# Projection A of a hybrid decoder layer as seven products of half blocks, with double-width evictions and a merge by halves of the tokens

## The chip, the cores and the metric

The kernel runs on one core of a Trainium2 chip. A core has a matrix engine (TensorE, PE in the profile; its weight loads are listed apart as PEld), a vector engine (VectorE, DVE), an activation engine (ScalarE, ACT), GpSimd (POOL) and a queue engine (SyncE, SP) that here only issues DMAs. Each engine works through its own list of instructions in order and waits on semaphores for the others. The metric is the device time of one execution in microseconds. Three runs of the kernel before took 1434.97, 1435.62 and 1437.99 us; the median is 1435.62 us.

## The reference, cut to what matters

One layer of a decoder trunk is computed for a prompt of 1024 tokens and for eight samples of one token, together 1032 columns. All data is float32.

```
h = rmsnorm(x, norm_pre) * (1 + scale) + shift
hA, cA, bA, zA, qkv, zB, beta_raw, alpha_raw, gA, gB = split(h @ w_in)
yA = ((bA * conv3(cA * hA)) * silu(zA)) @ w_out_a      # branch A, "projection A"
o  = gated_delta_rule(conv4(qkv), ...)                 # branch B, eight heads
yB = (rmsnorm(o) * silu(zB)) @ w_out_b                 # "projection B"
merged = sigmoid(gA) * yA + sigmoid(gB) * yB
y = x + gate * rmsnorm(merged @ w_o, norm_post)        # gate: from c @ ada_w, the "row gate"
```

The states of both convolutions and of the delta rule are outputs too.

## The kernel before, in words

Activations lie transposed: 128 channels on the partitions, 1032 tokens along the row (NT). A matrix of 1024 channels is eight such tiles. To keep float32 accuracy, each operand is split into a high part (a cast to float32r, on ACT) and a low part (the difference, on DVE), and each product of two tiles is three matmuls: high by high, high by low, low by high.

The stages, in order of time: a start with the norms; `run(jobs, 1, isp)`, the eight heads with the gates gA and gB, and the first three channel tiles of branch A; `products()`, the input tiles 3 to 7 of branch A; `products_b()`, projection B; `run(jobs, ioa, len(jobs))`, projection A; and the loop over nine row tiles with w_o, the last norm and the outputs. Results that a later stage needs (yA and yB before their projections, both gates) lie in DRAM: `yAsc`, `yBsc`, `gAsc`, `gBsc`.

`products()` and `products_b()` use the scheme of Strassen and Winograd on 2 x 2 blocks: a pair of output tiles by two halves of the tokens (HT = 516 columns) is made of seven products P1, P2, P6, P7, P4, P5, P3 (in that order), each of half as many input tiles. A product is taken in two pieces of PW = 258 columns, 12 matmuls each, and each piece is evicted from its PSUM bank by `evacuate`: ACT copies P1 to two quarters, DVE adds the others (two additions for P5, one for the rest). The weights of the products, some of them sums of blocks, are prepared by `weight_load` and `weight_gen`, one unit ahead; the operands of projection B by `yblock_gen`, at most three products ahead, from raw rows (P1, P2, P3) or from sums that `park_gen` has written to the DRAM tile `txs` (P6, P7, P4, P5), which come back through POOL's queue. In projection B a unit is a product with one of two weight groups; each unit serves two pairs of tiles.

Projection A before is plain: eight jobs, one for each output tile, of three groups of 344 columns and eight input tiles, three matmuls each. `load_rows` loads and splits the eight rows of yA, `oa_evac` multiplies each group by the sigmoid of gA and adds it to `mrg`, which holds the gated yB. While it runs, `side_gen` writes the convolution state of branch A and computes the row gate (32 matmuls of 512 columns, `rowgate_gen`), and `wo_gen` loads and splits w_o, tile by tile. The w_o loop starts with the sample tile (8 rows, `order = [8] + ...`), then the eight prompt tiles; `prep(j)` loads x and splits the columns of `mrg` for tile j, one tile ahead.

The order of instructions on each engine is written by a small planner while the program is built. Background work is a list of generators (strands). Between matmuls `slot()` advances every strand whose due time, worked out from costs written in the code, lies 450 ns behind the planner's clock of PE; `force(cond)` advances strands, and the clock with them, until a condition holds. A strand yields after each step, so that the next engine's step is written later. Nothing is reordered on the chip: an engine that comes to an instruction waits there. Buffers of a row's size come from a list (`T4`, 6 at first, 22 more for the products, 7 more from projection B on); `take` forces one free, `ready(n)` lets a strand wait for n. PSUM is eight banks in two pools of four.

Of the kernel before, what the change touches and what calls it, by code (L numbers as in the profile page):

```python
# [153 lines left out]
def hybrid_step(  # L154
# [22 lines left out]

    def tt(out, a, b, op):
        V.tensor_tensor(out=out, in0=a, in1=b, op=op)
# [94 lines left out]
    txs = dram.tile([2, 2, 4, P, NT], F32R, name="txs")  # L274
# [1013 lines left out]
    def conv_state_gen(branch):  # L1288
# [6 lines left out]
        for src, n, nt, o_p, o_s, row in (which,):  # L1295
            for t0 in range(0, nt, 4):
                pt = ps_aux()
# [13 lines left out]
    def rowgate_gen():  # L1311
        pt = [ps_aux(), ps_aux()]
# [34 lines left out]
    def side_gen():  # L1347
        yield from conv_state_gen("a")
        yield from rowgate_gen()

# [33 lines left out]
    UNITS = [(t, p, 0) for t in range(SG, NK) for p in PROD] + [("B", p, g) for p in PROD for g in range(2)]  # L1384

    def weight_load(raw):
        for key in list(range(SG, NK)) + ["B"]:
            w, n = (w_out_b, 2) if key == "B" else (w_in, 1)
            for odd, half in ((0, 0), (0, 1), (1, 0), (1, 1)):
                for g in range(n):  # L1390
                    yield from when(lambda: len(raw) < 4 * n, lambda: T4.ready())
# [38 lines left out]
    def park_gen():  # L1430

        for k in range(4):
            yield from when(lambda: T4.ready(2))
            a, b = T4.get("pa_", NT), T4.get("pb_", NT)
            SY.dma_start(out=a, in_=yBsc[k])
            SY.dma_start(out=b, in_=yBsc[4 + k])
            yield
            a1, a2, b1, b2 = a[:, 0:HT], a[:, HT:NT], b[:, 0:HT], b[:, HT:NT]
            tt(a1, a2, a1, ALU.subtract)
            tt(a2, b2, a2, ALU.subtract)  # L1440
            yield
            tt(b2, b2, a1, ALU.subtract)
            tt(b1, b1, b2, ALU.subtract)
            yield
            for r, v in enumerate((a, b)):
                yield from when(lambda: T4.ready(2))
                hi, lo = T4.get("phi", NT), T4.get("plo", NT)
                A.copy(out=hi.bitcast(F32R), in_=v)
                yield
                tt(lo.bitcast(F32R), v, hi, ALU.subtract)  # L1450
                T4.give(v)
                store(txs[r, 0, k].bitcast(F32), hi)
                store(txs[r, 1, k].bitcast(F32), lo)
                T4.give(hi)
                T4.give(lo)
                yield
        parked.append(True)

    parked = []
    yblk = {}  # L1460

    def yblock_gen():
# [109 lines left out]
    def products():  # L1572
# [3 lines left out]
        for t in range(SG, NK):  # L1576
            tiles = [T4.take("acc", NT) for _ in range(4)]
            for p in PROD:
# [6 lines left out]
                for q in range(2):  # L1585
                    ta, tb = tiles[2 * q:2 * q + 2]
                    for half in range(2):
                        ps = banks[4 * (n % 2) + 2 * q + half]
                        for k in range(4):
# [4 lines left out]
                            if k < 3:  # L1594
                                slot()
# [298 lines left out]
```

## Time and profile before

| | |
|---|---|
| median of three runs | 1435.62 us |
| the profiled execution's own time | 1434.01 us |
| its span, first to last instruction | 1432.3 us |
| mean granted clock of TensorE | 0.998 |
| PE, PEld busy | 98%, 94% of the span |
| DVE, ACT, POOL busy | 69%, 46%, 2% |
| DMA | 111 GB/s on average |
| products, from about 927 to 1147 us with the start of projection B's loads | PE full, DVE 82% up to 1128 us |
| projection B, 1147 to 1228 us | DVE 59.69 us busy |
| projection A, 1227.5 to 1326.7 us | DVE 59.45 us busy |
| w_o, from 1326.7 us | 93.2 us of matmuls without a pause, then 7.7 us to the end |

Times are microseconds unless marked ns, counted from the start of the span. A row of a group gives line, engine, operation, output and input tiles, shapes and count, then the busy time, the mean duration in ns and the idle time before the group with what ended it. All instructions carry the line of the planner's wrapper, L121, so groups are told apart by their tiles. `pm_t` and `pa_t` are the two PSUM pools. Matmuls overlap in the array: the time that one costs is the distance between two starts, not its duration. A few matmul records are missing from the trace.

### The profile page before, as it was taken

The numbers are of one execution on the slowest core, as the hardware profiler recorded it, in microseconds if no ns is written. First come the engines' busy times: TensorE is split into PE (matmuls) and PEld (weight loads), VectorE is DVE, ScalarE is ACT, GpSimd is POOL, SyncE is SP. The second block draws the span as 40 slices with busy tenths as digits, with TensorE's granted clock in tenths as the row PEclk, the third lists the DMA queues.
The fourth block names the chain that finished last, engine by engine and source line by source line (L and its number), as shares of the span: only waits on it lengthen the run. The fifth ranks groups of instructions, "written<-read, shape, count | busy, mean of one in ns | idle before, by whom it ended". The sixth has DMA issues, their size and how long they took to land.

```text
span 1432.3 us, 25802 instructions
## 1 busy us (share of the span) xinstructions
PE 1401.0 (98%) x10130; PEld 1340.5 (94%) x10130; DVE 984.4 (69%) x2436; ACT 656.4 (46%) x1521; POOL 35.6 (2%) x59
## 2 busy tenths in 40 slices
PE   6999999899999999999999999999999999999997
PEld 4899999899999999999999999999999999999786
DVE  6754867759569585496864924988877867854553
ACT  6766453855528554466383332253323344532211
POOL 0000000100001000000000000000000110000000
PEclk9999999999999999999999999999999999999999
DMA  9523143132422324224132221344711885743221
GB/s 320 144 48 102 54 127 81 54 80 78 119 60 69 94 62 117 50 66 121 54 97 68 79 68 32 118 170 164 243 53 42 236 265 172 244 150 91 92 87 59
DMA packets 181922, 158.59 MB, mean 111 GB/s; under 512 B 25351, under 2 KB 157856, under 8 KB 181794
## 3 DMA queue, kind: packets, MB, share of 16 engines
q1 hardware_dynamic: 177248, 148.43, 35.2%
q0 software_dynamic: 4352, 8.46, 2.0%
q8 instruction: 79, 1.29, 0.4%
q14 instruction: 41, 0.34, 0.1%
q10 hardware_dynamic: 202, 0.08, 0.0%
HBM read 120.25 MB, written 36.91 MB: 110 GB/s over the span
## 4 chain that ended last, share of the span: by engine, by line
PE 84%; DVE 8%; DMA 5%; ACT 1%; issue 1%; SPq 1%; DVEq 0%; ACTq 0%
PE pm_t L121 63%; PE pa_t L121 19%; PE pb L121 2%; DVE acc L121 2%; DVE wlo L121 1%; DMA xs<-in_x_prompt_dram 1%; SPq L121 1%; DMA yraw<-yAsc 1%; DVE Tt L121 1%; DVE kq L121 1%; DMA wor<-in_w_o_dram 1%; DVE Ttmp L121 1%; DVE wr L121 0%; DMA yraw<-yBsc 0%; DMA pa__11678<-yBsc 0%
## 5 line engine op out<-in xcount | busy, mean ns | idle before, releaser
L121 PE MATMUL pm_t<-xh,whi 128*128 128x344 f32 (+1 forms) x1576 | 517.9, 329 | 2.2 <-ACT gate L121 2.2
L121 PE MATMUL pm_t<-xh,wlo 128*128 128x344 f32 (+1 forms) x1576 | 500.4, 318 | 0.0
L121 PE MATMUL pm_t<-xl,whi 128*128 128x344 f32 (+1 forms) x1576 | 500.1, 317 | 0.0
L121 PEld LDWEIGHTS pm_t<-xh,whi 128*128 128x128 f32 x1576 | 297.4, 189 | 4.7 <-ACT gate L121 2.5
L121 PEld LDWEIGHTS pm_t<-xl,whi 128*128 128x128 f32 x1576 | 297.3, 189 | 0.2
L121 PEld LDWEIGHTS pm_t<-xh,wlo 128*128 128x128 f32 x1576 | 296.9, 188 | 0.4
L121 DVE TENSOR_TENSOR wlo<-wraw,whi 128x512 fp32r<-128x512 f32 x136 | 91.8, 684 | 65.2 <-ACT whi L121 63.1
L121 ACT CAST whi<-wraw 128x512 fp32r<-128x512 f32 x136 | 82.7, 623 | 85.6 <-PE pm_t L121 83.6
L121 DVE TENSOR_TENSOR Ttmp<-Tt 32x30 f32<-32x30 f32 (+14 forms) x240 | 76.1, 317 | 14.7 <-DMA Tt<-sA 10.3
L121 DVE TENSOR_TENSOR Tt<-Tt,Ttmp 32x30 f32<-32x30 f32 (+14 forms) x240 | 76.2, 317 | 4.4
L121 ACT CAST whi<-wr 128x1024 fp32r<-128x1024 f32 x42 | 44.0, 1047 | 73.5 <-PE pa_t L121 34.9
L121 DVE SCALAR_TENSOR_TENSOR kq<-raw,vecs,kq 128x528 f32<-128x528 f32 x96 | 69.9, 758 | 1.5 <-ACT kq L121 1.3
L121 PE MATMUL pm_t<-thi,wlo 128*128 128x258 f32 x240 | 67.6, 283 | 1.6 <-DVE wlo L121 1.6
L121 PE MATMUL pm_t<-tlo,whi 128*128 128x258 f32 x240 | 67.6, 282 | 0.0
L121 PE MATMUL pm_t<-thi,whi 128*128 128x258 f32 x240 | 67.6, 282 | 0.0
L121 PE MATMUL pa_t<-thi,whi 128*128 128x258 f32 x224 | 63.3, 282 | 1.1 <-ACT whi L121 1.1
L121 PE MATMUL pa_t<-thi,wlo 128*128 128x258 f32 x224 | 63.4, 283 | 0.8 <-DVE wlo L121 0.8
L121 PE MATMUL pa_t<-tlo,whi 128*128 128x258 f32 x224 | 63.2, 282 | 0.0
L121 PE MATMUL pm_t<-yhi,whi 128*128 128x344 f32 x192 | 61.5, 321 | 0.0
L121 PE MATMUL pm_t<-ylo,whi 128*128 128x344 f32 x192 | 61.4, 321 | 0.0
L121 PE MATMUL pm_t<-yhi,wlo 128*128 128x344 f32 x192 | 61.4, 320 | 0.0
L121 DVE TENSOR_TENSOR wlo<-wr,whi 128x1024 fp32r<-128x1024 f32 x42 | 51.3, 1221 | 8.9 <-ACT whi L121 8.7
(406 smaller groups left out, 2834.0 us busy)
## 6 DMA issues: line engine op xcount, KB each, us to landing
wraw<-in_w_in_dram SPq DMA_DIRECT2D x60, 512.0 KB
wr<-in_w_in_dram SPq DMA_DIRECT2D x40, 256.0 KB
aw<-in_ada_w_dram SPq DMA_DIRECT2D x16, 512.0 KB
gBsc<-gate SPq DMA_DIRECT2D x8, 516.0 KB
gAsc<-gate SPq DMA_DIRECT2D x8, 516.0 KB
txs<-phi SPq DMA_DIRECT2D x8, 516.0 KB
txs<-plo SPq DMA_DIRECT2D x8, 516.0 KB
tlo<-txs POOLq DMA_DIRECT2D x8, 516.0 KB, 7.3
```

What stands on the lines that cost most here:

```text
L121: r = f(*args, **kw)
```

## The change

Projection A gets the scheme of projection B: `products_b` becomes `products_y(y)` and runs for "B" and then for "A"; weights, parked sums and operand blocks are made for both, with a DRAM tile `txs` for each. The products of A are accumulated in eight row buffers.

PSUM is divided anew from `products()` on: three tiles of two banks each for the products, and two single banks for the row gate and the state of branch A. Both pieces of a product lie in the two banks of one tile and are evicted by one instruction of 2 x 258 columns (`product`).

The gate of A works by halves of the tokens (`merge_gen`): sigmoid of half a row, product with half an accumulator, addition to `mrg`. The first halves start after P4, the second after P5 and P3.

The row gate moves from projection A into `products()`, behind the parking of B and ahead of the parking of A; the state of branch A moves to P4 of projection A, as does the start of `wo_gen`, which also waits until the last operand block is out. The w_o loop takes the prompt tiles first and the sample tile last; the first four prompt tiles ask only for merged first halves, and leave slots for background work.

```diff
-    def side_gen():
-        yield from conv_state_gen("a")
-        yield from rowgate_gen()
+    def side_gen():
+        for k in range(4):
+            yield from park_gen("B", k)
+        yield from rowgate_gen()
+        for k in range(4):
+            yield from when(lambda: ("yA", 4 + k) in flags)
+            yield from park_gen("A", k)
...
     def products():
-        start(park_gen())
-        banks = [ps_main() for _ in range(4)] + [ps_aux() for _ in range(4)]
+        psum["pm"].release()
+        psum["pa"].release()
+        psum["pp"] = tc.alloc_tile_pool(name="pp", bufs=3, space=PSUM)
+        psum["pr"] = tc.alloc_tile_pool(name="pr", bufs=2, space=PSUM)
+        start(side_gen())
...
+    def product(p, whi, wlo, k0, operands, ta, tb):
+        ps = psum["pp"].tile([P, 2, 512], F32, tag="pp", name="pp")
+        for half in range(2):
+            out = ps[:, half, 0:PW]
+            for k in range(4):
+                xh_, xl_ = operands[4 * half + k]
+                PE.matmul(out, lhsT=whi[:, k0 + k, :], rhs=xh_, start=k == 0, stop=False)
+                PE.matmul(out, lhsT=whi[:, k0 + k, :], rhs=xl_, start=False, stop=False)
+                PE.matmul(out, lhsT=wlo[:, k0 + k, :], rhs=xh_, start=False, stop=k == 3)
+                if k < 3:
+                    slot()
+            if half == 0:
+                slot()
+        v = ps[:, :, 0:PW]
+        C11, C12, C21, C22 = (t_[:, o:o + HT].rearrange("p (h n) -> p h n", h=2) for t_ in (ta, tb) for o in (0, HT))
         if p == "P1":
             A.copy(out=C11, in_=v)
             A.copy(out=C12, in_=v)
         for out, in_ in {"P1": (), "P2": ((C11, C11),), "P6": ((C12, C12),), "P7": ((C22, C12),),
                          "P4": ((C21, C22),), "P5": ((C22, C22), (C12, C12)), "P3": ((C12, C12),)}[p]:
             tt(out, v, in_, ALU.add)
...
+    def merge_gen(t, half):
+        yield from when(lambda: T4.ready())
+        s_ = T4.get("sg", NT)
+        hs = slice(half * HT, half * HT + HT)
+        sg, acc_ = s_[:, 0:HT], T["acc", t][:, hs]
+        SY.dma_start(out=sg, in_=gAsc[t, :, hs])
+        yield
+        act(sg, sg, AF.Sigmoid)
+        yield
+        tt(acc_, acc_, sg, ALU.mult)
+        T4.give(s_)
+        yield from when(lambda: ("gate", t) in flags, lambda: half == 0 or ("merged", t, 0) in flags)
+        tt(T["mrg"][:, t, hs], T["mrg"][:, t, hs], acc_, ALU.add)
+        flags["merged", t, half] = True
+        if half:
+            T4.give(T["acc", t])
+
+    def products_y(y):
         for p in PROD:
             for g in range(2):
...
+                if y == "A" and p == "P4" and g:
+                    start(conv_state_gen("a"))
+                    start(wo_gen())
...
+                    product(p, whi, wlo, 4 * q, xs_, ta, tb)
+                    if y == "B" and p in ("P5", "P3"):
+                        t = 2 * i + (p == "P5")
+                        start(gate_gen(t))
+                    elif y == "A" and p in ("P4", "P5", "P3"):
+                        for t, half in {"P4": ((2 * i, 0), (2 * i + 1, 0)), "P5": ((2 * i + 1, 1),),
+                                        "P3": ((2 * i, 1),)}[p]:
+                            start(merge_gen(t, half))
...
     def wo_gen():
         for t in range(NK):
-            yield from when(lambda: T4.ready(3 if flags.get("rg") else 6))
+            yield from when(lambda: T4.ready(3), lambda: flags.get("yblocks"))
...
-    products_b()
-    run(jobs, ioa, len(jobs))
+    products_y("B")
+    products_y("A")
     force(lambda: flags.get("rg") and all(("wo", t) in T for t in range(NK)))
...
-    order = [8] + list(range(8))
+    order = list(range(8)) + [8]
...
     def prep(j):
         i = order[j]
         n = P if i < 8 else NB
-        xr = S_.get("xr", D)
+        force(lambda: all(("merged", t, int(i > 3)) in flags for t in range(NK)))
+        xr = S_.take("xr", D)
...
+                if j < 4:
+                    slot()
```

More of the change, by code (lines that the diff above doesn't have):

```diff
@@ L1585, in products @@
                 for q in range(2):
[L1586 to L1589, printed above, removed]
[L1590 to L1598 removed]
+                    xs_ = [operand(p, k, half) for half in range(2) for k in range(4)]
+                    product(p, whi, wlo, 4 * q, xs_, *tiles[2 * q:2 * q + 2])
                 if t == NK - 1 and p in ("P6", "P7", "P4"):
```

234 lines of the change are left out of this document (85 added, 149 removed).

## The prediction

> **What bounds the kernel now.** I read the first page for the shares, then a table of stretches for the end of the kernel, then the matmuls, the vector engine and the waits inside these stretches.
>
> ```profile
> span 1432.3 us, 25802 instructions
> PE 1401.0 (98%) x10130; PEld 1340.5 (94%) x10130; DVE 984.4 (69%) x2436; ACT 656.4 (46%) x1521; POOL 35.6 (2%) x59
> 927.00:1128.00 201.00, 199.68 (x1638) 199.15 (x1637) 164.49 (x255) 73.81 (x105) 0.83 (x1) 1.00 0.44 140
> 1147.00:1228.00 81.00, 78.68 (x651) 77.95 (x650) 59.69 (x96) 39.19 (x53) 4.90 (x7) 1.00 0.68 220
> 1227.50:1326.70 99.20, 99.20 (x617) 95.71 (x616) 59.45 (x87) 34.91 (x43) 0.00 (x0) 1.00 0.50 156
> 1326.70:1331.40 4.70, 3.83 (x18) 1.68 (x16) 4.42 (x6) 2.27 (x4) 0.00 (x0) 1.00 0.66 232
> 1331.40:1424.60 93.20, 93.18 (x400) 73.88 (x400) 43.73 (x131) 17.65 (x41) 0.00 (x0) 1.00 0.20 68
> ```
>
> The columns of the stretches: length, then PE, PEld, DVE, ACT and POOL busy, granted clock, DMA share, GB/s. They are the products of branch A's input tiles 3 to 7, projection B, projection A, the seam, and w_o. PE never rests for more than a moment, so time is won only by fewer or shorter matmuls, and lost wherever PE begins to wait. DVE is the second engine: 82% (164.49 of 201) in the products, 74% in projection B, 60% in projection A, 47% in w_o. That last row is what I watch, since the change moves vector work between these stages.
>
> **The matmuls of projection A.** Busy times overlap, so the pace is read from start to start.
>
> ```profile
> 1249.16 0.63 PE L121 MATMUL pa_t<-rg_h,cP 128*64 128x512 f32 x2
> 1249.62 0.63 PE L121 MATMUL pa_t<-rg_l,cP 128*64 128x512 f32 x2
> 1250.09 0.32 PE L121 MATMUL pm_t<-yhi,whi 128*128 128x344 f32 x1
> ...
> 1255.93 0.32 PE L121 MATMUL pm_t<-ylo,whi 128*128 128x344 f32 x1
> 1198.64 5.75 PE pa_t L121 x48
> 1204.39 5.82 PE pm_t L121 x48
> ```
>
> From 1250.09 to 1255.93 are 38 matmuls of 344 columns, 37 steps: 5.84/37 = 157.8 ns. In projection B (the chain's last two rows) 48 matmuls of 258 columns take 1204.39-1198.64 = 5.75 us: 119.8 ns. Removed: 8 tiles x 3 groups x 8 x 3 = 576 x 157.8 ns = 90.9 us. Added: 4 pairs x 7 products x 2 halves x 4 x 3 = 672 x 119.8 ns = 80.5 us. **Saved: 10.4 us.** The columns fall to 7/8 (672 x 258 of 576 x 344), which would be 79.5 us; the shorter matmul costs a little more a column, 0.464 ns against 0.459. The row gate's 32 matmuls (0.93 us for four, 7.4 us) go from this stage into the products: nothing won, nothing lost on PE. The same holds for the transposes of the conv state.
>
> **What DVE has to do at the end of projection A.** The merging of the two branches, which stood spread over the 99 us of projection A, may begin only with product P4, and the splits of w_o only behind P4's first half as well. From there to the first complete w_o tile DVE's price decides. Three rows of projection B give its pace back to back, two more the single durations.
>
> ```profile
> 1207.07 1.42 DVE L121 TENSOR_TENSOR mrg<-pm_t,mrg 128x258 f32<-128x258 f32 x4
> 1208.41 1.22 DVE L121 TENSOR_TENSOR mrg<-mrg,sg 128x1032 f32<-128x1032 f32 x1
> 1209.55 1.46 DVE L121 TENSOR_TENSOR mrg<-pm_t,mrg 128x258 f32<-128x258 f32 x4
> L121 DVE TENSOR_TENSOR tlo<-qb,thi 128x516 fp32r<-128x516 f32 x5 | 3.5, 690 | 0.0
> L121 DVE TENSOR_TENSOR wol<-wor,woh 128x1024 fp32r<-128x1024 f32 x8 | 9.8, 1223 | 7.1 <-ACT woh L121 7.1
> ```
>
> Four evictions of 258 columns take 1.34 us to the next start, 0.335 each; one of 1032 takes 1.14. On the line between them 516 columns cost 0.603 and 1024 cost 1.13. Queued on DVE from the start of P4 until the first tile's low part is made: 17 evictions (4 of P4, 8 of P5, 4 of P3, the last of P7) x 0.603 = 10.3; 5 weight splits x 1.13 = 5.7; 2 splits of P3's operand x 1.14 = 2.3; 16 half merges of two operations x 0.603 = 19.3; 8 splits of w_o x 1.13 = 9.0; one split of the tile, 1.1. **Sum 47.7 us.** PE has 12 products x 24 x 119.8 ns = 34.5 us in that time. At its start DVE also rests: the first merge waits for a product (2.9 us), half of a load that took 4.89 us (the row below) and a sigmoid, 5.9 us together, and only 3.5 us of other work are at hand: 2.4 us. So PE, whose third matmul of w_o reads that low part, waits 47.7+2.4-34.5 = 15.6 us, or 13.2 if the last two half merges (2.4) come behind; I take **14.4**. With whole durations in place of the pace (0.69, 1.22 and 1.23) the sum is 53.4 and the wait 21.3, the upper end. The lower end is 3.5: all 8 merges of the second half (9.7 us) behind the first tile, no rest. Evictions wait in this same queue, so PE may pay a part of it inside P5 and P3; the sum stays.
>
> Merging two evictions into one saves a fixed cost each time, 2 x 0.335-0.603 = 67 ns by the rows. The Trainium skill (Perfetto Trace Analysis, section Optimizing Scalar/DVE Operations) puts DVE's fixed cost at about 60 ns on SBUF and about 125 ns on PSUM. By the page each of the 17 evictions would take some 60 ns more, 1.0 us in all, and the time would be 1445.0. The trace disagrees: the PSUM rows above run with 67 ns.
>
> **The other terms.**
>
> ```profile
> PE pa_t L121 <- ACT whi L121: 1.1, 1, 1.1
> PE pa_t L121 <- DVE wlo L121: 0.8, 1, 0.8
> PE pm_t L121 <- DVE wlo L121: 0.4, 1, 0.4
> PE pm_t L121 <- DVE wlo L121: 1.2, 1, 1.2
> PE pm_t L121 <- DVE cP L121: 0.9, 1, 0.9
> 1318.31 4.89 DMA sg<-gAsc
> ```
>
> These are PE's waits: the first three in projection B, where weights come late behind the four sums of P2; the fourth in the products; the fifth at the seam. Projection A now runs the same chain of weights with the same sums: **+2.3** (bounds 0 and twice that). The seam's 0.9 goes with the sample tile: **-0.9**.
>
> ```profile
> 500.00:503.00 3.00, 1.79 (x13) 1.51 (x11) 0.19 (x2) 0.04 (x1) 0.00 (x0) 1.00 0.37 98
> 503.00:506.50 3.50, 2.71 (x13) 2.71 (x14) 3.19 (x15) 0.27 (x1) 0.00 (x0) 0.73 0.00 0
> 506.50:512.00 5.50, 5.50 (x35) 5.50 (x35) 4.47 (x16) 3.08 (x12) 0.00 (x0) 0.86 0.04 6
> ```
>
> After a stretch in which PE worked 1.79 of 3.00 us the granted clock fell to 0.73 and 0.86: 0.27 x 3.5 + 0.14 x 5.5 = 1.7 us lost. A wait of 14 us should do it too: **+1.7** (0 if the wait is short).
>
> ```profile
> 1424.68 0.60 ACT L121 ACTIVATE sqj<-pm_t 128x512 f32<-128x512 f32 x1 [4.97 <-PE pm_t L121]
> L121 ACT COPY sqj<-pm_t 8x512 f32<-8x512 f32 x2 | 1.2, 577 | 2.5 <-PE pm_t L121 2.5
> L121 DVE TENSOR_TENSOR sqj<-sqj,pm_t 8x512 f32<-8x512 f32 x2 | 1.4, 676 | 2.0 <-ACT sqj L121 2.0
> L121 DVE COPY yt<-sqj 8x512 f32<-8x512 f32 x2 | 0.8, 416 | 0.1
> ```
>
> The sample tile, now last, has three steps ahead of the squaring that the prompt tile (first row) hasn't: 577+676+416 ns = 1.7 us; its store has 8 rows in place of 128, for which I take 0.4 back, an estimate: **+1.3** (bounds 0 and 1.7).
>
> The rest I cost at nothing, with its cover.
>
> ```profile
> L121 DVE TENSOR_TENSOR rg_l<-rg_r,rg_h 128x1024 fp32r<-128x1024 f32 x8 | 9.8, 1220 | 2.5 <-ACT rg_h L121 2.5
> ```
>
> In the products DVE gains the row gate's 8 splits (9.8 us) and its end (about 3 such operations, 3.7) and loses 4.7 by 70 evictions in place of 140: 173 of 208 us, still 83%; SP's queue gets 8 loads of 512 KB past the weight loads at 140 GB/s. If a row gate's matmul stands in PE's queue before its split is done, the nearest row is 1.2 us, eight times 9.6. Parking y_A (4 x 4.7 us of DVE, 8 loads, 16 stores on SP, 16 more loads on POOL's queue, all due 23 us or more later) falls into the end of the products and into projection B, where it takes the place of eight row splits and raises 59.7 of 81 us to some 75 at most; 0 to 3 us if it makes weights late. ACT, 35 of 99 us busy in projection A, covers the sigmoids, half as long each and twice as many, and the casts.
>
> Sum: -10.4-0.9+2.3+14.4+1.7+1.3 = **+8.4 us** on the profiled execution's 1434.0, 1442.4. The median of the runs shown is 1.6 above that execution: **1444.0**.
>
> **The rivals.** *The second half steps aside* (the other sign). The code asks only for first-half merges before tile 0, and the first four w_o tiles leave places for background work. If the planner puts the 8 second-half merges there, the wait is 3.5 to 5.9: -10.4-0.9+3.5+1.3 = -6.5, or with the rest, the late weights and the slow clock -0.1; 1429.1 to 1435.5, middle 1432.3. It decides where less than 44.5 us of DVE work (34.5+10.4+0.9-1.3, nothing else lost) precedes the tile. Against it: before that tile stands a demand for all eight w_o splits, and while the planner walks towards the last of them, the merges, due earlier, are written too.
>
> *The w_o chain runs one tile at a time.*
>
> ```profile
> 1305.81 3.67 DMA wor<-in_w_o_dram
> 1310.58 1.24 DVE wol L121
> 1311.83 3.69 DMA wor<-in_w_o_dram
> ```
>
> Load, cast and split took 6.02 us a tile there, the next load behind the last split. From some 14 us after P4's start (P3's second operand must be out first) eight such steps end at 62: a wait of 28.8 with the tile's split, 14.4 more than forecast, 1458. Against it: these were the last loads of a crowded stage; later some 13 of 35 buffers are free (8 hold accumulators, 8 operands, 2 weights, about 4 loads of gates), and loads can go ahead.
>
> *The PSUM ring.* Three pairs of banks let an eviction be 2 x 2.9 = 5.75 us late, eight banks 7 x 1.44 = 10. If the bursts of finish_group break this once in each of five tiles by the 1.2 us of the nearest row, +6: 1450. Against it: no PSUM wait in the rows.
>
> **How the numbers follow.** Chances: the forecast 0.52, second half aside 0.28, the serial chain 0.12, the ring 0.08. The forecast's own range is 1439 to 1452 (waits of 10 to 21, small terms with them). 1430 to 1453 leaves out a quarter of the second rival (0.07) and the serial chain (0.12). What a measurement can tell from no change is 0.2%, 2.9 us: 1432.7 to 1438.5. Faster: two thirds of "aside", 0.18. Same: its rest and the forecast's lower edge, 0.14. Slower: 0.68.
>
> **What would show it.** After: 258-column matmuls at 119.8 ns in projection A and its 80.5 us plus waits; DVE over 90% busy from P4 to w_o's start; PE's longest wait there, on ml or on acc's evictions, 13 to 16 us in sum, clock below 1 behind it; the last rows those of 8x512. Wrong, if PE enters w_o without a wait, or if it waits on loads of w_o.

## The result and the profile after

The changed kernel takes 1460.31 us, the median of four runs from 1459.61 to 1461.56; four runs of the kernel before beside them took 1434.97 to 1437.99, median 1435.67. The ratio is 1.017, with a 95% interval from 1.0152 to 1.0187: slower by 24.6 us. The profiled execution took 1459.62 us, its span 1457.9.

From the first page of the changed kernel, its span and the busy time of each engine:

```profile
span 1457.9 us, 26057 instructions
PE 1402.4 (96%) x10226; PEld 1336.1 (92%) x10226; DVE 1020.6 (70%) x2378; ACT 670.5 (46%) x1513; POOL 47.0 (3%) x75
```

PE is as long busy as before (1402.4 against 1401.0 us) in a span that is 25.6 us longer. That does not mean that the shorter matmuls won nothing. By the two tables below PE's busy time falls by 17.6 us in projection A, of which the row gate took 7.4 along, and the remaining 10 come back as the same matmuls running longer: 6.0 us more in projection B and 4.8 more from the seam on, where the granted clock is lower. In sum the longer span is PE's pauses. The tables of stretches, cut at the first matmul of each stage, say where they are. Columns: length; then PE, PEld, DVE, ACT and POOL busy; granted clock, DMA share, GB/s. The kernel before (products, projection B, projection A with the row gate, seam with the sample tile, the other w_o matmuls, tail):

```profile
940.40:1143.50 203.10, 201.78 (x1682) 201.25 (x1681) 165.87 (x262) 71.95 (x101) 3.69 (x5) 1.00 0.50 154
1143.50:1227.20 83.70, 81.38 (x674) 80.76 (x674) 62.69 (x99) 40.53 (x52) 7.89 (x11) 1.00 0.67 216
1227.20:1326.70 99.50, 99.50 (x620) 96.01 (x619) 59.45 (x87) 34.97 (x43) 0.00 (x0) 1.00 0.50 156
1326.70:1335.60 8.90, 8.03 (x35) 4.00 (x34) 6.26 (x10) 3.83 (x8) 0.00 (x0) 1.00 0.36 124
1335.60:1424.20 88.60, 88.60 (x383) 71.56 (x381) 41.89 (x127) 16.09 (x38) 0.00 (x0) 1.00 0.21 72
1424.20:1432.30 8.10, 0.38 (x2) 0.00 (x0) 3.67 (x13) 0.69 (x2) 0.00 (x0) 0.83 0.17 65
```

The changed kernel (products with the row gate, projection B, projection A up to P7 and from P4 on, seam, w_o up to the last low-part matmul of a prompt tile, tail with the rest of the sample tile):

```profile
942.40:1152.00 209.60, 209.03 (x1713) 205.90 (x1714) 170.51 (x205) 79.51 (x91) 1.55 (x2) 1.00 0.53 166
1152.00:1250.80 98.80, 87.40 (x682) 85.47 (x681) 76.84 (x90) 41.32 (x44) 10.03 (x14) 0.95 0.94 308
1250.80:1300.00 49.20, 47.14 (x386) 46.40 (x385) 33.60 (x37) 18.53 (x26) 10.02 (x14) 1.00 0.75 217
1300.00:1335.80 35.80, 34.81 (x290) 34.59 (x288) 32.97 (x48) 18.53 (x24) 1.44 (x2) 1.00 0.63 199
1335.80:1348.30 12.50, 2.66 (x6) 1.01 (x5) 12.50 (x15) 4.32 (x5) 0.00 (x0) 0.62 0.62 196
1348.30:1442.00 93.70, 93.66 (x390) 73.24 (x391) 39.01 (x116) 15.99 (x36) 0.00 (x0) 0.98 0.21 74
1442.00:1457.90 15.90, 5.51 (x23) 2.33 (x21) 9.66 (x32) 3.28 (x8) 0.00 (x0) 0.79 0.10 35
```

| stage | before | after | difference | predicted |
|---|---|---|---|---|
| start of the products | 940.4 | 942.4 | +2.0 | 0 |
| products, with the row gate after | 203.1 | 209.6 | +6.5 | +7.4 |
| projection B | 83.7 | 98.8 | **+15.1** | 0 (up to 3) |
| projection A | 99.5 | 85.0 | -14.5 | -15.5 |
| from its end to the end | 105.6 | 122.1 | +16.5 | +16.5 |

Projection B, whose matmuls are the same before and after, holds the surprise. PE works 87.40 of 98.80 us there, at a granted clock of 0.95 (0.05 x 98.8 = 4.9 us lost), while the DMA engines went from a share of 0.67 to 0.94. The two longest of PE's waits in it (waiting, releaser; us in total, times, longest), and then two pieces of the chain of work that ended last (start, length):

```profile
PE pp L121 <- DMA thi<-txsB: 4.7, 1, 4.7
PE pp L121 <- ACT mrg L121: 2.9, 2, 2.4
```

```profile
1152.18 10.83 DMA yraw<-yBsc
...
1199.50 14.32 DMA thi<-txsB
```

A row load of y_B, the last of the four that P1 and P2 need, was asked for at 1152.18, when projection B had just begun, and landed 10.83 us later. In the kernel before the last of the four was asked for at 1126.50, 17 us ahead of projection B. In SyncE's list now two loads of the parking (at 1148.67 and 1149.21) and two of weights stand right ahead of it. What that does is seen in ACT's own list, with its idle time and what ended it in brackets:

```profile
1163.03 1.05 ACT L121 CAST thi<-yraw 128x1032 fp32r<-128x1032 f32 x1 [6.10 <-DMA yraw<-yBsc]
1163.99 1.04 ACT L121 CAST whi<-wr 128x1024 fp32r<-128x1024 f32 x1
```

ACT stood for 6.10 us at the cast of that row. The cast of the next weights and the evictions of P1 (`mrg`) stood behind it, and PE waited for an eviction (2.42 us, at 1166.06). The row itself was late too: P2 began at 1166.1, and PE waited 1.8 us for its low part, up to 1171.51. The other late place is POOL's queue. Its last load in the kernel before, and then its last loads after, for the operands of P4 and P5:

```profile
1161.69 0.72 POOL L121 DMA_DIRECT2D tlo<-txs  x1 [5.61 <-issue]
```

```profile
1196.97 0.71 POOL L121 DMA_DIRECT2D thi<-txsB  x1 [8.86 <-DVE pb__13702 L121]
1198.08 1.43 POOL L121 DMA_DIRECT2D tlo<-txsB  x2 [0.40 <-issue]
1199.50 1.45 POOL L121 DMA_DIRECT2D thi<-txsB  x2
```

The queue was through at 1161.69, 18 us into projection B; now its last loads are asked for from 1196.97 on, 45 us into it. P4 begins at 1208.3, and the load issued at 1199.50 lands 14.32 us later, by the chain above, at 1213.82.

At the seam PE's list, and what DVE did meanwhile, show what was forecast. PE stands for 3.64, 2.87 and 3.38 us with two matmuls after each of the first two waits, and DVE works without a gap through the last merges, six splits of w_o and the splits of the first tiles:

```profile
1335.73 0.28 PE L121 MATMUL pp<-thi,wlo 128*128 128x258 f32 x1
1339.65 0.80 PE L121 MATMUL po<-woh,mh 128*128 128x512 f32 x1 [3.64 <-ACT mh L121]
1340.24 0.63 PE L121 MATMUL po<-wol,mh 128*128 128x512 f32 x1
1343.74 0.80 PE L121 MATMUL po<-woh,mh 128*128 128x512 f32 x1 [2.87 <-ACT mh L121]
1344.34 0.63 PE L121 MATMUL po<-wol,mh 128*128 128x512 f32 x1
1348.34 0.79 PE L121 MATMUL po<-woh,ml 128*128 128x512 f32 x1 [3.38 <-DVE ml L121]
```

```profile
1339.05 1.29 DVE L121 TENSOR_TENSOR mrg<-mrg,acc 128x516 f32<-128x516 f32 x2
1340.26 6.89 DVE L121 TENSOR_TENSOR wol<-wor,woh 128x1024 fp32r<-128x1024 f32 x6
1347.07 2.35 DVE L121 TENSOR_TENSOR ml<-mrg,mh 128x1024 fp32r<-128x1024 f32 x2
```

### The profile page after: what moved, and what is told of

It is laid out like the page before. It is cut to its first block, busy times and chain, and to the rows that moved or that the text cites. A ratio compares the mean times of both kernels' runs of the same rounds, so it can differ in the third digit from the quotient of the medians.

```text
span 1457.9 us, 26057 instructions
## 1 busy us (share of the span) xinstructions
PE 1402.4 (96%) x10226; PEld 1336.1 (92%) x10226; DVE 1020.6 (70%) x2378; ACT 670.5 (46%) x1513; POOL 47.0 (3%) x75
## 4 chain that ended last, share of the span: by engine, by line
PE 84%; DVE 7%; DMA 6%; ACT 1%; issue 1%; SPq 0%; POOL 0%; DVEq 0%; ACTq 0%; POOLq 0%
PE pm_t L121 47%; PE pp L121 16%; PE pa_t L121 13%; PE po L121 7%; PE pb L121 2%; DVE wlo L121 1%; DVE mrg L121 1%; DMA sg<-gAsc 1%; DVE acc L121 1%; DMA thi<-txsB 1%; DMA yraw<-yBsc 1%; DMA xs<-in_x_prompt_dram 1%; DMA aw<-in_ada_w_dram 1%; DVE wol L121 1%; DVE kq L121 1%
## 5 line engine op out<-in xcount | busy, mean ns | idle before, releaser
L121 PE MATMUL pm_t<-xh,whi 128*128 128x344 f32 x1416 | 472.6, 334 | 2.2 <-ACT gate L121 2.2
L121 PE MATMUL pm_t<-xh,wlo 128*128 128x344 f32 x1416 | 455.1, 321 | 0.0
L121 PE MATMUL pm_t<-xl,whi 128*128 128x344 f32 x1416 | 455.0, 321 | 0.0
L121 PE MATMUL pp<-thi,whi 128*128 128x258 f32 x688 | 196.4, 286 | 7.8 <-DMA thi<-txsB 4.7
L121 PE MATMUL pp<-thi,wlo 128*128 128x258 f32 x688 | 196.3, 286 | 4.4 <-DVE wlo L121 4.4
L121 PE MATMUL pp<-tlo,whi 128*128 128x258 f32 x688 | 196.1, 285 | 2.7 <-DVE tlo L121 2.7
L121 PEld LDWEIGHTS pp<-thi,whi 128*128 128x128 f32 x688 | 131.7, 191 | 9.3 <-DMA thi<-txsB 4.9
L121 PEld LDWEIGHTS pp<-thi,wlo 128*128 128x128 f32 x688 | 131.6, 192 | 5.7 <-DVE wlo L121 5.6
L121 PEld LDWEIGHTS pp<-tlo,whi 128*128 128x128 f32 x688 | 131.9, 192 | 3.4 <-DVE tlo L121 3.2
L121 PE MATMUL pp<-xh,whi 128*128 128x258 f32 x320 | 90.5, 283 | 0.5 <-ACT szA L121 0.5
L121 DVE TENSOR_TENSOR wlo<-wr,whi 128x1024 fp32r<-128x1024 f32 x54 | 65.8, 1220 | 11.1 <-ACT whi L121 11.1
```

Of the source, the lines that this page charges most:

```text
L121: r = f(*args, **kw)
```

## The experiments

Two questions: is the seam DVE's queue, and why is projection B late? Every kernel is the changed one with the edit shown. A time without an interval is one execution. The kernel before ran beside each group on the same chip and took 1437.5, 1436.0, 1438.0, 1434.6 and 1439.0 us beside the five groups below (medians of seven, but one execution each beside the third and fourth). "B" is the time from the first matmul of projection B to the first of projection A; the seam is the time from the last matmul of projection A to the first of w_o that reads a low part. In the runs without the parking, or with only a part of it, projection A reads sums that are not its own, so branch A of their result is not the layer's; only their times count.

### First group: the seam, and the parts of the parking

**defer**, the second halves' merges behind the first w_o tile:

```diff
     def merge_gen(t, half):
-        yield from when(lambda: T4.ready())
+        yield from when(lambda: T4.ready(), lambda: half == 0 or flags.get("tile0"))
...
     prep(0)
+    flags["tile0"] = True
```

> The eight merges of the tokens' second half wait until the first w_o tile has been split; the result is unchanged. Theory: the 12.6 us between the last matmul of projection A and the third of w_o are vector work in front of that tile's low part; 8 merges x 1.21 us = 9.7 us go behind it, so the gap shrinks to 3 to 5 us and the slow clock behind it goes too: 9 to 12 us faster than the changed kernel, about 1449. Rival: the gap is the chain of loading and splitting w_o one tile at a time; then it stays at 10 to 13 us and the time at 1457 to 1460.

Measured: 1450.97 us (1450.29 to 1454.07), ratio to before 1.010 (1.0083 to 1.0117). The seam fell from 12.5 to 6.7 us. Two stretches of this run, from the start of P4 and from the end of projection A:

```profile
1298.30:1332.90 34.60, 34.60 (x290) 34.54 (x288) 32.04 (x42) 15.05 (x16) 1.44 (x2) 1.00 0.60 185
1332.90:1339.60 6.70, 2.03 (x7) 1.49 (x5) 6.67 (x11) 2.75 (x4) 0.00 (x0) 0.84 0.87 296
```

DVE works 38.7 us in place of 45.5, and the seam shrinks by 5.8: the seam is DVE's queue, not the loads of w_o. It shrank by less than the 9.7 us that were expected: of the sixteen operations of the second halves ten stand behind the first low part now, and six still ahead of it; one split of w_o went behind it as well. The total fell by 9.3; the other 3.5 are not of the seam (B 96.8 in place of 98.8, projection A 83.4 in place of 85.0).

**no_park**, no parking of y_A at all; **no_store**, without its stores; **raw_store**, without its arithmetic:

```diff
no_park:    side_gen
-        for k in range(4):
-            yield from when(lambda: ("yA", 4 + k) in flags)
-            yield from park_gen("A", k)
+        parked["A"] = 4
no_store:   park_gen
+            if y == "B":
                 store(txs[y][r, 0, k].bitcast(F32), hi)
                 store(txs[y][r, 1, k].bitcast(F32), lo)
raw_store:  park_gen, behind the loads
+        if y == "A":
+            for r, v in enumerate((a, b)):
+                store(txs[y][r, 0, k].bitcast(F32), v)
+                store(txs[y][r, 1, k].bitcast(F32), v)
+                T4.give(v)
+                yield
+            parked[y] = parked.get(y, 0) + 1
+            return
no_park, no_store:   yblock_gen
-                                         in_=txs[y][r, part, kk:kk + 2, :, cs]
+                                         in_=txs["B"][r, part, kk:kk + 2, :, cs]
```

> The parking of y_A is left out whole: P6, P7, P4 and P5 of projection A take projection B's parked sums, so the result of branch A is wrong; all matmuls, evictions and loads of blocks stay. Theory: parking (12.7 MB of transfers, 18.8 us of vector work) is what made projection B take 98.8 us instead of 83.8; without it projection B falls to 82 to 86 us and the whole by 13 to 17 us, to about 1445. Rival: the three pairs of PSUM banks and the chain of weights cost it whatever is parked; then projection B stays above 94 us and the whole above 1455.

> Parking of y_A keeps its 8 loads and all of its arithmetic, but its 16 stores (8.5 MB) are left out and the sums of projection B are read in their place, so branch A is wrong. If the traffic decides: projection B falls to 84 to 90 us, total 1446 to 1452. If DVE's and ACT's share of parking decides: projection B stays at 95 to 99 us, total above 1456.

> Parking of y_A keeps its 8 loads and 16 stores but leaves out its 16 subtractions and 8 splits (18.8 us of DVE, 8.4 us of ACT); unsummed rows are stored twice, so branch A is wrong. If the traffic decides: projection B stays at 93 to 99 us. If the arithmetic decides: it falls to 84 to 88 us, total 1446 to 1450.

Measured: B 87.7, 96.5 and 99.4 us (totals 1457.91, 1456.98, 1460.4). So the parking is 11.1 of the 15.1 us, but neither its stores nor its arithmetic alone: each can go and B stays late. Without the parking projection A lost 5.9 us (85.0 to 90.9; PE waits there 5.8 us for weights, and 3.0 us for weights and an operand in the changed kernel), and the start and the end from w_o on were 1.6 and 1.5 longer, so the total fell by far less than B.

### Second group: bytes, buffers, the row gate

```diff
no_park_few:         no_park, and
-    T4.extend(alloc("m2", "right"), "sr", NSR, NT)
+    T4.extend(alloc("m2", "right"), "sr", NSR - 4, NT)
no_park_gate_last:   no_park, and the row gate from the first unit of projection A on
+        yield from when(lambda: flags.get("A"))
         yield from rowgate_gen()
traffic:             no_park, and in the place of the parking
+            for i in range(6):
+                store(..., gAsc[i + 2 * (k % 2)])
gate_in_a_defer:     defer, the parkings of A right behind those of B, then
+        yield from when(lambda: flags.get("A"))
+        yield from rowgate_gen()
```

> The parking of y_A is left out as before, and the last extension of the buffer list has 3 rows in place of 7, from projection B on: about as many as the parking held (two raw rows and up to two parts). If the buffers it held make projection B late, B rises from 87.7 to 95 us or more, with POOL waiting on reused buffers; if not, B stays within 3 us of 87.7.

> The parking of y_A is left out as before, and the row gate starts with projection A in place of the products. If the row gate in the products costs PE nothing but its own 7.4 us, the products fall from 209.9 to 202 to 203.5 us, projection B stays at 84 to 88 us, projection A rises by 7 to 8 from 90.8 to 98 or 99. If the row gate's loads and buffers are what is left late in projection B (3.9 us over before), B falls to 84.

Measured: with four rows of buffer fewer B took 81.9 us (total 1450.83), so scarce buffers are not the cause. With the row gate out of the products these took 201.2 in place of 209.9 us, and B 83.8 (total 1451.23). The products of the second run:

```profile
944.80:1146.00 201.20, 201.20 (x1681) 201.20 (x1682) 160.51 (x193) 70.01 (x80) 2.98 (x4) 1.00 0.50 153
```

PE never rests through all 35 products (35 x 5.75 = 201.3 us). The row gate had cost 8.7 us for 7.4 us of matmuls. Without it the products took 1.9 us less than in the kernel before (203.1), whose PE waited there 1.2 us once for the low part of a weight. Whether the double-width evictions won this is not shown, since PSUM and the order changed with them.

> The parking of y_A is left out as in the run without it (projection A reads the sums of y_B; its result is wrong in those four products), and 24 copies of 516 KB from DRAM to DRAM, gate rows to a place nobody reads, are issued at the same places of SyncE's queue: the bytes of the parking, without its buffers, its work on DVE and ACT and without a consumer. If the moved bytes make projection B late, B is again 95 to 100 us and the DMA share there 1.0 or more; if buffers or queue places do, B stays at 85 to 90 us as without the parking (87.7).

Measured: B 88.0, total 1453.33. The run says nothing of bytes, and something else instead. SyncE's list in the stage of the heads, hundreds of microseconds before the place where the copies were written:

```profile
560.85 0.33 SPq L121 DMA_DIRECT2D gAsc<-gate  x1
562.10 0.37 SPq L121 DMA_DIRECT2D wraw<-in_w_in_dram  x1
564.10 2.37 SPq L121 DMA_DIRECT2D txsA<-gAsc  x4
```

The copies stand right behind the stores of the gates that they read. All 24 were issued between 469 and 760 us, long before the products. What the planner writes late is not necessarily late in the built program: the build had moved these transfers ahead, to where the rows that they read had been stored. (The description of the kernel before said that the planner sets the order; for the queues that is only the order in which they are written.) As a repetition of the kernel without the parking it agrees with it, 88.0 against 87.7.

The runs without the parking also show where the 4.0 us lie by which B is still longer than before. In no_park PE has two waits in B, 4.3 us for `whi` and 0.5 for `wlo`. ACT's list there, and then the same place in the kernel before:

```profile
1189.56 1.28 ACT L121 ACT_TABLE_LOAD   x1 [11.38 <-DMA sg<-gBsc]
```

```profile
1170.93 1.28 ACT L121 ACT_TABLE_LOAD   x1 [5.77 <-DMA sg<-gBsc]
...
1173.20 1.03 ACT L121 CAST whi<-wr 128x1024 fp32r<-128x1024 f32 x1
```

The sigmoid of gate B (the load of its table stands first) waits for a gate row, and the cast of the next weights stands behind it. In traffic PE waits 4.5 us for these weights, in no_park_gate_last 1.8, in no_park_few not at all, and B takes 88.0, 83.8 and 81.9 us. In the kernel before it waits 1.1 us. In the changed kernel this wait is not among PE's: the parking makes other loads the late ones, so the 11.1 and the 4.0 us are differences between runs and not two waits of one run.

> Whole computation. The row gate starts with projection A, the parkings of A stand right behind those of B, the merges of the second half wait until the first w_o tile is prepared. Theory (late loads in B because the parking's 12.7 MB come when B's own are due): most of the parking now lies in the products, where the DMA share was 0.44 before; products 202 to 204 us, B 86 to 90, projection A 92 to 94 with the row gate's 7.4, seam 6 to 8, w_o and tail 109: 1440 to 1446. If the parking costs the same wherever it stands, B stays at 95 to 99 or the products rise: 1449 to 1452.

Measured: 1470.19 us, ratio 1.0236 (1.0211 to 1.0262); products 204.6, B 109.2. This is far from what was expected (1440 to 1446). ACT's list 10 us into B:

```profile
1156.14 1.28 ACT L121 ACT_TABLE_LOAD   x1 [5.99 <-DMA sg<-gAsc]
...
1158.93 1.06 ACT L121 CAST whi<-wr 128x1024 fp32r<-128x1024 f32 x1
```

Loads of gate A, meant for the end of projection A, had been moved into B's start, and their sigmoid stands ahead of B's weights: the same picture as with `yraw`, with another load. It is not the whole of it: gate_in_a below, without the deferred merges, still takes 102.9.

### Third group: own buffers, and bytes alone

```diff
own_buf:    pa_, pb_, phi, plo of A's parkings in four rows that nothing else uses until the end
traffic2:   the copies of traffic read what is stored late
+                store(..., yAsc[6 + (k > 0)])
best1:      own_buf and defer, and
-    order = list(range(8)) + [8]
+    order = [0, 1, 2, 3, 8, 4, 5, 6, 7]
```

> Whole computation. The parking of y_A takes four rows of the buffer list for itself (raw a, raw b, high part, low part), uses them for all four of its steps and gives them back at the end; no load of projection B reuses a row in which the parking still works. If the reuse is what makes B late (its POOL loads waited 8.9 us on such a row and 0.9 on another), B falls from 98.8 to 86 to 91 us and the wait on P4's operand goes. If the moved bytes or the parking's places in the engines' queues do, B stays at 95 us or more.

> The parking of y_A is left out (projection A reads the sums of y_B in four of its products), and 24 copies of 516 KB from DRAM to DRAM stand in SyncE's queue, 6 behind the store of y_A's tile 6 and 18 behind that of tile 7, so that their 12.4 MB move between 1115 and 1220 us, where the parking's did; no buffer, no ACT or DVE work, no consumer. If the bytes make B late: 95 us or more, DMA share above 1.0 from 1170 on. If not: 82 to 90 us, as in the three runs without the parking (87.7, 88.0, 81.9).

Measured: with own rows B took 98.1 us (total 1457.6); which row a load reuses is not the cause, though it is what the wait on `pb__13702` had suggested. With the 24 copies and nothing else of the parking B took 100.5 (total 1466.57):

```profile
1151.90:1252.40 100.50, 88.31 (x677) 86.75 (x676) 65.87 (x74) 36.00 (x39) 10.04 (x14) 0.93 0.92 293
```

So transfers alone are enough, without a buffer and without work on DVE or ACT. It need not be their bytes: SyncE itself waits among the copies, 4.4 us for the store of y_A that they read and 16.0 us for copies issued before, by the waits that the profile gives for its queue.

> Whole computation; three edits together: the parking of y_A in four rows of its own, the merges of the second half behind the preparation of the first w_o tile, the sample tile fifth in place of last. If the reuse of rows is the cause in B: 1436 to 1443 (products 209, B 88, projection A 85, seam 6.8, w_o 100, tail 8 us, start 943). If not, 10 us more: 1446 to 1453.

Measured: 1458.7, above the 1446 to 1453 expected; B 102.8, seam 7.1, w_o 100.4, tail 8.1. With the sample tile fifth, w_o and tail take 108.5 us, with it last 109.6; from the last matmul to the end it is 8.1 against 9.3.

### Fourth group: how many bytes, and when

```diff
traffic_half:   12 copies
-            for i in range(6):
+            for i in range(0, 6, 2):
loads_only:     the edit of yblock_gen above, and in park_gen, behind the loads
+        if y == "A":
+            T4.give(a)
+            T4.give(b)
+            parked[y] = parked.get(y, 0) + 1
+            return
half_park:      park_gen stores one float32 row for each sum; yblock_gen splits it
+            if y == "A":
+                store(txs[y][r, 0, k].bitcast(F32), v)
gate_in_a:      gate_in_a_defer without the deferred merges
```

> As the run with 24 copies of 516 KB behind the stores of y_A's tiles 6 and 7 (parking left out, four products of projection A read the sums of y_B), but with 12 copies, 6.2 MB. If B's lateness grows with the bytes that move beside its own: 90 to 95 us, between no copies (87.7, 88.0, 81.9) and 24 copies (100.5). If it is the mere presence of the copies in SyncE's queue: 98 to 101.

> Of the parking of y_A only the 8 loads stay (4.2 MB); its arithmetic on DVE and ACT and its 16 stores are left out, and four products of projection A read the sums of y_B. With the arithmetic and without the stores B took 96.5 us. If there DVE's work behind late loads was the cause, B is now 85 to 91 us; if the loads' bytes and places in the queue were, B stays at 94 to 97.

> Whole computation with half of the parked bytes: each sum of y_A is stored once as a float32 row (8 stores in place of 16) and split when projection A loads it (8 more splits on ACT and DVE there, 2 of them behind P4). If bytes decide: B 91 to 95 us in place of 98.8, projection A 85 to 88, seam 12.6 to 15, total 1455 to 1460. If DVE's and ACT's places in the queue decide as much as the bytes: B 95 to 98.

> Whole computation; the row gate starts with projection A, the parkings of A stand right behind those of B, three of the four in the products, where the DMA share was 0.44 before; the merges are as in the changed kernel. If bytes beside B's own make it late, moving 9.5 of 12.7 MB out of it brings B to 86 to 92 us, products 203, projection A 92 to 95; total 1447 to 1453. In the run with the merges held back as well B took 109.2, with four loads of gate A and the sigmoids behind them standing in SyncE's and ACT's queues between B's weights; if those were not to blame, B stays above 100.

Measured: B 98.4, 94.3, 94.1 and 102.9 us; totals 1463.56, 1461.9, 1458.59 and 1471.77. Loads alone, without stores and arithmetic, still make B late (94.3), and so does half of the stores (94.1, as expected). The size of the delay does not go by the bytes: half the copies cost almost what all cost, and with three of four parkings stored before B it was worse (102.9, where 86 to 92 was expected). Where the half of the copies hurt is again ACT's list:

```profile
1203.32 1.28 ACT L121 ACT_TABLE_LOAD   x1 [20.47 <-DMA sg<-gBsc]
...
1205.58 1.03 ACT L121 CAST whi<-wr 128x1024 fp32r<-128x1024 f32 x1
```

A load of gate B, asked for at 1192.93 behind the copies, held the sigmoid, and this held the weights of P7's second unit: P7's first unit took 19.2 us in place of 5.75. In gate_in_a ACT stands 15.05 us at the same place, and PE waits 8.1 for the weights. That leaves the order as the suspect: which transfers stand ahead of B's own, and what stands behind them on ACT.

### Fifth group: the parking behind B's own loads

```diff
late_park:   side_gen
-            yield from when(lambda: ("yA", 4 + k) in flags)
+            yield from when(lambda: ("yA", 4 + k) in flags,
+                            lambda: len(yblk.get(("B", "P4"), ())) == 2 or flags.get("late"))
+            flags["late"] = True
best3:       late_park, the sample tile fifth, and in merge_gen, with half rows sharing a buffer
         act(sg, sg, AF.Sigmoid)
-        yield
+        yield from when(lambda: half == 0 or flags.get("tile0"))
```

> Whole computation; the only edit is that the parking of y_A waits until the operand blocks of projection B's product P4 have been asked for, so that all loads of w_out_b, four of the six row loads of y_B and the loads of the parked sums of y_B up to P4 stand ahead of it in the queues. If B is late because its own loads share queue places and bytes with the parking's, B falls from 98.8 to 85 to 91 us, and projection A (85.0) loses 0 to 6 by sums that are parked late: total 1449 to 1455. If any transfer beside B makes it late wherever it stands, B stays at 94 to 100.

Measured: B 90.0 us, projection A 89.5, total 1457.96 (1449 to 1455 was expected). Two stretches of B, its first twelve units and its last two, and then the first twelve units of the changed kernel:

```profile
1153.60:1222.60 69.00, 69.00 (x578) 69.00 (x577) 58.70 (x71) 28.94 (x32) 9.32 (x13) 1.00 1.02 338
1222.60:1243.60 21.00, 15.64 (x106) 14.86 (x105) 18.43 (x22) 10.10 (x11) 0.00 (x0) 0.84 0.69 242
```

```profile
1152.00:1239.20 87.20, 75.80 (x587) 73.95 (x585) 65.24 (x76) 35.09 (x38) 10.03 (x14) 0.94 0.99 325
```

This is the clearest pair of rows of the study. For 69 us PE works without a gap, twelve units at 5.75, while the DMA engines are as full as they were in the changed kernel in the same twelve units, which took 87.2 us (share 1.02 and 338 GB/s against 0.99 and 325). So full DMA engines did not stop PE here. What changed is the order: the last row load of P2 is asked for at 1139.44, 14 us ahead of projection B in this run, and not at its start. The gain does not all stay. P3's first unit takes 15.3 us: PE waits 3.0 for the low part of its operand and 2.4 for evictions. DVE's list there holds gates (7.3 of 18.43 us), evictions (4.7) and splits of weights and rows (7.3); the parking's own operations are 2.6, so that the parking is what pushed P3 back was not shown. Projection A loses 4.5 us.

> Whole computation; the late parking, the sample tile fifth in place of last, and the multiplications and additions of the second-half merges written behind the preparation of the first w_o tile, their loads and sigmoids at their old place. If late parking cures B: products 209, B 88, A 86, seam 7 to 13, w_o 100.4, tail 8.1 from 943: 1441 to 1448, still above before's 1435. If not: 1450 to 1458.

Measured: 1454.82 us, ratio 1.0105 (1.0078 to 1.0132), where 1441 to 1448 was expected if late parking cures B. It did: B took 90.3 us, as in late_park. The seam is 0.5 us, but w_o takes 114.2 in place of 100.4 with the same tile order: PE enters w_o before the splits of w_o are done and waits inside it, for `ml` (3.8 us), `wol` (3.2) and `ms` (2.1). (The profiled execution, from which the stages are, was the longest of four, 1460.31.) Of the versions that compute the whole layer the shortest is defer with 1450.97; against the kernel before beside each, defer and best3 are not told apart (1.010 and 1.0105), and none reaches it.

## Why the prediction was right and wrong

It forecast 1444.0 us in a range from 1430 to 1453. The direction was right and the time fell outside.

- **The matmuls of projection A: right.** 258-column matmuls in place of 344-column ones, -10.4 us, less 2.3 for late weights and 7.4 for the row gate: -15.5 forecast, -14.5 measured. The excess over 80.5 us is 4.5 in place of 2.3, with 3.0 of waits for low parts of weights and of an operand in it.
- **DVE at the end of projection A: right, and in its own terms.** 47.7 us of work and 2.4 of rest, less 2.4 if the last merges come behind, should set the time from P4's start to the matmul of w_o that first reads a low part, 34.5 + 14.4 = 48.9. It was 1348.3 - 1300.0 = 48.3, with DVE busy 32.97 + 12.50 = 45.5 and 2.8 at rest. PE lost 1.3 of it before the seam, so the seam itself was 12.5, and its named waits add up to 9.9, not 13 to 16. That the middle of the two sums was met so closely is partly luck: no merge came behind the tile, but six of the 32 merge operations stood ahead of P4, at 1279 to 1300 us. The prediction let none begin before P4; by the code the first half of an even tile needs only P1 and P2. The run with the deferred merges moved the time the right way, by 5.8 of the 9.7 us of the sum. One size in the sum can be checked, the fixed cost of an eviction. DVE's list 10 us before the seam has a pair from PSUM (`pp`) and then operations on SBUF:

```profile
1325.96 1.29 DVE L121 TENSOR_TENSOR acc<-pp,acc 128x516 f32<-128x516 f32 x2
1327.17 1.29 DVE L121 TENSOR_TENSOR mrg<-mrg,acc 128x516 f32<-128x516 f32 x2
1328.38 0.69 DVE L121 TENSOR_TENSOR acc<-acc,sg 128x516 f32<-128x516 f32 x1
```

  Both pairs take 1.21 us from start to start, 0.605 each. The Trainium skill (Perfetto Trace Analysis, section Optimizing Scalar/DVE Operations) has the fixed cost on PSUM at twice that on SBUF; the trace of the changed kernel disagrees. The prediction's own 67 ns was weaker than it says, since its 0.603 lay on a line between one PSUM row and one SBUF row; with 0.605 measured from PSUM it is 2 x 0.335 - 0.605 = 65 ns.
- **The slow clock behind the wait: right** in size. The stretch of w_o has a mean clock of 0.98: 0.02 x 93.7 = 1.9 us, forecast 1.7.
- **The sample tile at the tail: right**, +1.1 (109.6 against 108.5 in best1) for +1.3. The 0.4 us that it took back for the smaller store had no row behind it; from DVE's last operation to the end of the span it came out at 2.5 us, against 3.0 in the kernel before.
- **The row gate at nothing beyond its 7.4 us: nearly.** It cost 8.7 there, and the products without it were 1.9 shorter than before.
- **The step that failed: parking y_A**, which "falls into the end of the products and into projection B", was costed at nothing, with "0 to 3 us if it makes weights late". It made B 11.1 us longer, and the whole change 15.1. The step weighed the busy time of DVE ("59.7 of 81 us to some 75 at most", and 76.84 it was) and counted the DMAs, 8 loads and 16 stores, but found them harmless because their own data was due 23 us later. What it did not ask is whose transfers stand behind them, and what stands behind those on ACT and DVE. The runs showed this in its place: lateness of a load in B passes through ACT's and DVE's lists to weights and evictions whose own data was there. A sign of it stood in the prediction, which read the waits of 1.1 and 0.8 us in projection B as weights that come late behind the four sums of P2. By the lists of the kernel before no sum stood there: ACT had stood 5.77 us at the sigmoid of gate B, for its load, with the cast of those weights behind it.
- **The rest of B's 15.1**, the 4.0 us that stay without the parking, went when the row gate left the products as well (83.8) but also when rows were taken away (81.9). In the trace it is the same pattern as in the kernel before, only longer: ACT's wait for a load of gate B, with weights behind it. Why that load comes at another time in each of the four builds without the parking, whose B ranges over 6 us, was not shown. A slow clock is in the 15.1 too, 4.9 us by the row of the stage.
- **The rivals.** The second half did not step aside, and w_o's loads did not run one at a time: DVE did six splits without a pause (6.89 us, shown above). The PSUM ring was named for the products, where PE lost less than 1 us; in B two waits on `mrg`, 2.9 us, are of its kind, brought on by ACT's wait for a row.

Summed by stages, the forecast for the profiled execution was 1442.4 and the measurement is 1459.6; of the 17.2 between, 15.1 are projection B.

**What stays open:** why B takes 94 us in one order and 109 in another. For the builds whose lists are shown, which load stood ahead of which was read in the trace afterwards and predicted for none. That the order is the cause rests on late_park and best3 (90.0 and 90.3 us with most of the parking still in B, against 81.9 to 88.0 without it and 94.1 to 109.2 in every other version that has the parking, a part of it or the late copies) and on the lists of ACT. Late parking moves loads, stores and arithmetic together, and a run that moves one single load, or only the sigmoid of gate B behind the weights, was not made.

## What to carry to other kernels

When work is moved into a stage that is bound by PE, count the transfers that will stand ahead of the stage's own loads, and then read on each engine what stands behind an instruction that waits for a load: on ACT a cast or a sigmoid held the cast of weights that stood behind it. Ask of a wait in the profile before, even one of 1 us, what stood ahead on the engine that ended it. Adding up an engine's queue from a fixed start to a fixed need, with back-to-back durations, gave the 48.3 us from P4 to w_o to within 1 us; a share of busy time gave none of the 15 us in B. Look up the order in the built program, not the one in the source, before a step is called harmless.

## What the runs showed of the hardware that was not expected

DMA engines at a share of 1.02, 338 GB/s, left PE at 69.00 of 69.00 us; at 0.99 and 325 GB/s, in another order, the same twelve units took 87.2. A pause in B also costs twice: the granted clock of the stage fell to 0.95 after waits of 5 us and less, and a unit of P4, whose own wait was 4.7 us by PE's table, took 13.1 in place of 5.75, at a granted clock of 0.74. At the seam the clock was still low once PE worked again without a gap:

```profile
1348.30:1352.30 4.00, 3.96 (x9) 3.13 (x10) 1.33 (x3) 0.00 (x0) 0.00 (x0) 0.50 0.42 125
1352.30:1360.00 7.70, 7.70 (x34) 6.03 (x33) 0.75 (x2) 0.69 (x2) 0.00 (x0) 1.00 0.01 2
```

The Trainium skill (TensorE: Matmul & The Clock Gate, section What's actually happening) has the clock at half after an idle window of some 3.4 us and at full speed after about as long a stretch of work. The rows agree on the way up: 4.0 us at 0.50, then 1.00. On the way down less was enough here. Around the start of P2 in projection B PE waited 2.4, 0.5 and 1.8 us between 1163.6 and 1171.5, with matmuls between, and from 1171.51 to 1173.50 the granted clock was 0.50.
